# A copy-bound rotation kernel: the first two stores cut into 2 KB pieces

## The chip, the cores and the metric

The kernel runs on one core of a Trainium2 chip. The metric is the time of one execution on the device in microseconds (us), quoted as the median of several runs. The span of a profiled run is the time from its first to its last instruction. Engines named below are VectorE (DVE in the profile), ScalarE's queue (ACTq, which issues the stores here), SyncE's queue (SPq, which issues the loads), and the 16 DMA engines that move the bytes.

All differences here are below 2%, most below 0.5%, so every experiment was timed in five rounds beside runs of the kernel before on the same chip (both_short and loads_short have four timings on record, the others five).

## The reference, cut to what matters

```python
batch, c, h, w = 32, 3, 256, 256
x = np.random.randn(batch, c, h, w).astype(np.float32)

def reference(x):
    return np.rot90(x, k=-1, axes=(-2, -1)).astype(np.float32)
```

Every image of 256 x 256 is rotated by 90 degrees. There is no arithmetic: 25.17 MB are read, rearranged and written.

## The kernel before

The work is cut into 24 slabs of 1 MB. A slab lies on 128 partitions with 2048 floats, 8 KB, in each. A slab is loaded, transposed by two VectorE instructions, and stored. Loads are issued by SyncE and stores by ScalarE, and the trace has them on two DMA queues, of 25.17 MB each: q1 has the loads (first packet at 1.8 us) and q10 the stores (first packet at 13.9 us).

```python
R = 8
n_slabs = B * C * G // P          # 24
PARTS = 2
CP = R // PARTS
...
in_pool = ctx.enter_context(tc.tile_pool(name="in_pool", bufs=12))
out_pool = ctx.enter_context(tc.tile_pool(name="out_pool", bufs=12))

for n in range(n_slabs):
    t_in = in_pool.tile([P, R * W], fp32, tag="t_in")
    nc.sync.dma_start(out=t_in, in_=ld_v[n])

    t_out = out_pool.tile([P, R * W], fp32, tag="t_out")
    src = t_in.rearrange("p (r g c) -> p c r g", r=R, c=R)
    dst = t_out.rearrange("p (c g r) -> p c r g", c=R, r=R)[:, :, ::-1, ::-1]
    for k in range(PARTS):
        cs = slice(k * CP, (k + 1) * CP)
        nc.vector.transpose(out=dst[:, cs], in_=src[:, cs])

    nc.scalar.dma_start(out=st_v[n], in_=t_out)
```

## Time and profile before

| | before |
|---|---|
| time, median (range) | 124.83 us (124.66 to 124.93, 6 runs) |
| span of the profiled run | 122.9 us |
| moved | 50.34 MB, half read from and half written to HBM |
| VectorE busy | 94.6 us (77%) |
| DMA engines | full from the second slice to the last but one, at about 427 GB/s |

The lines below are from the profile's page of the kernel before: the busy digits of VectorE and of the DMA engines in 40 slices of 3.07 us, the traffic in each slice, and the packet count.

```profile
DVE  0199999999897697796977967979769779797500
...
DMA  2999999999999999999999999999999999999994
GB/s 93 427 427 403 339 424 427 427 429 427 427 432 427 427 427 427 432 429 427 427 427 427 429 427 427 427 427 429 427 427 427 427 429 427 427 429 427 427 424 171
DMA packets 6913, 50.34 MB, mean 410 GB/s; under 512 B 768, under 2 KB 768, under 8 KB 768
```

The DMA row is at 9 almost everywhere while VectorE has gaps, so data movement is the bound. And "busy" is not "at full rate": in the slices 4 and 5 the DMA row still shows 9 but only 403 and 339 GB/s move. The same stretch in windows of 1 us (columns: window, its length, busy time of VectorE and of GpSimd with their instruction counts, granted clock, DMA busy share, GB/s; a packet counts whole in the window in which it starts, so a share can exceed 1):

```profile
11.00:12.00 1.00, 1.00 (x2) 0.00 (x0) 1.00 0.94 360
12.00:13.00 1.00, 1.00 (x1) 0.00 (x0) 1.00 1.06 311
13.00:14.00 1.00, 1.00 (x2) 0.00 (x0) 1.00 0.96 287
14.00:15.00 1.00, 1.00 (x1) 0.00 (x0) 1.00 0.94 393
```

This is where the stores join the loads. The first store was issued at 9.67 us and its first packet starts at 13.9 us. Against 427 GB/s, 323 of the 357 GB/s x us that are missing lie before 14 us, so it is the loads that lose, before the first store packet is on record. I call this the dip. Who waited for whom on VectorE (columns: waiter, what it waited for, us in total, times, longest):

```profile
DVE t_out L51 <- DMA t_in<-in_x_dram: 15.4, 12, 5.7
DVE t_out L51 <- DVE t_out L51: 5.4, 6, 0.9
```

### The profile page before, as it was taken

What the parts mean: (1) busy time and instruction counts of PE and PEld (TensorE: products, weight loads), DVE (VectorE), ACT (ScalarE), POOL (GpSimd) and SP (SyncE); (2) the same over time, 40 slices, a digit from 0 to 9 for tenths busy, and PEclk for the clock granted to TensorE, in tenths of its full rate; (3) what the DMA queues carried; (4) which work ended last, traced back from release to release, by engine and by line L of the source; (5) the groups of instructions that cost most, each with busy time, mean ns of one, the idle gap of its engine ahead of it and who ended that gap; (6) DMA issues with size and microseconds to landing.
All of it is one profiled execution on the core that took longest, in us unless ns stands there. A gap on an engine that the chain in (4) does not pass through costs nothing.

```text
span 122.9 us, 186 instructions
## 1 busy us (share of the span) xinstructions
DVE 94.6 (77%) x48; POOL 0.2 (0%) x4
## 2 busy tenths in 40 slices
DVE  0199999999897697796977967979769779797500
POOL 0000000000000000000000000000000000000000
DMA  2999999999999999999999999999999999999994
GB/s 93 427 427 403 339 424 427 427 429 427 427 432 427 427 427 427 432 429 427 427 427 427 429 427 427 427 427 429 427 427 427 427 429 427 427 429 427 427 424 171
DMA packets 6913, 50.34 MB, mean 410 GB/s; under 512 B 768, under 2 KB 768, under 8 KB 768
## 3 DMA queue, kind: packets, MB, share of 16 engines
q1 hardware_dynamic: 3456, 25.17, 49.2%
q10 hardware_dynamic: 3456, 25.17, 48.5%
q14 instruction: 1, 0.01, 0.0%
HBM read 25.17 MB, written 25.17 MB: 410 GB/s over the span
## 4 chain that ended last, share of the span: by engine, by line
DMA 89%; DVE 2%; DVEq 2%; SPq 1%; issue 0%
DMA t_in<-in_x_dram 89%; DVE t_out L51 2%; DVEq L79 2%; SPq L44 1%; DVEq L51 0%
## 5 line engine op out<-in xcount | busy, mean ns | idle before, releaser
L51 DVE STREAM_TRANSPOSE t_out<-t_in 128x1024 f32<-128x1024 f32 x48 | 94.6, 2052 | 20.9 <-DMA t_in<-in_x_dram 15.4
L68 POOL MEMSET const-uint8-127<- 128x1 uint8 x1 | 0.1, 102 | 0.0
L68 POOL MEMSET const-bfloat16-1.0<- 128x1 bf16 x1 | 0.1, 101 | 0.0
L68 POOL MEMSET const-float32-0.0<- 128x1 f32 x1 | 0.1, 98 | 0.2 <-issue 0.2
L68 POOL MEMSET const-float32-1.0<- 128x1 f32 x1 | 0.1, 98 | 0.0
## 6 DMA issues: line engine op xcount, KB each, us to landing
t_in<-in_x_dram SPq DMA_DIRECT2D x24, 1024.0 KB, 19.6
out_dram<-t_out ACTq DMA_DIRECT2D x24, 1024.0 KB, 16.5
```

The source lines that it names most:

```text
L44: nc.sync.dma_start(out=t_in, in_=ld_v[n])
L51: nc.vector.transpose(out=dst[:, cs], in_=src[:, cs])
L68: nc = _bacc.Bacc("TRN2", target_bir_lowering=False, num_devices=1)
L79: with _tile.TileContext(nc) as tc:
```

## The change

The first two stores are to go out as 512 packets of 2 KB each instead of 128 packets of 8 KB; a packet is what the trace records as one transfer of a DMA engine, and `max_dma_last_dim` limits its length in bytes. The likely intent is that the early loads get ahead of the early stores. The limit of 8 KB on the other stores changes nothing, as their rows are 8 KB long.

```diff
     PARTS = 2
+    SHORT = 2
...
-        nc.scalar.dma_start(out=st_v[n], in_=t_out)
+        nc.scalar.dma_start(out=st_v[n], in_=t_out,
+                            max_dma_last_dim=2048 if n < SHORT else 8192)
```

## The prediction

> **What bounds the kernel now.** The data movement. The page gives 50.34 MB in a span of 122.9 us, and in its 40 slices the DMA row is at 9 from the second slice to the last but one, at about 427 GB/s; VectorE is busy 94.6 us (77%). The chain of waits is 89% loads. In the trace nearly every 8 KB packet took 309 ns, 26.5 GB/s on one of 16 engines, 424 GB/s on all. 50.33 MB at 427 GB/s are 117.9 us. The other 5 us are: about 1.8 us before the first load packet, a ramp of the first loads (packets of 350 to 540 ns until about 2.8 us), a dip at the first store, and 1.3 us after the last store packet at 121.6 us.
>
> The dip is the only loss that the change can reach. In windows of 1 us the traffic is 360, 311, 287 and 393 GB/s from 11 to 15 us; load packets take up to 640 ns there. Against 427 this loses 357 GB/s x us, or 0.84 us. The first store was issued at 9.67 us, but its first packet starts only at 13.9 us.
>
> **What the change does.** A row of a store is 8 KB, so the limit of 8 KB on stores 2 to 23 changes nothing. Stores 0 and 1 become 512 packets of 2 KB each instead of 128 of 8 KB: 768 more packets, 48 on each engine. The 4-byte semaphore packets took 9 ns, so I estimate (309-9)/4+9 = 84 ns for 2 KB, and 48 x 9 ns = 0.43 us of additional engine time. Engine time is the bound, so this lies wholly on the critical path.
>
> **What it moves.** [...] loads get about 4/5 of the bytes while the short stores run: the mixed traffic of one load and one store packet is 309 + 84 ns. Stores 0 and 1 would then land much later (the first lands at 19.3 us now; I expect 25 to 30, the second 35 to 40), loads 4 to 10 sooner (near 3.2 to 3.5 us apart instead of 4.9), and VectorE would run without waits in that stretch. Stores pile up and drain at the end: the last loads land some 8 to 12 us before the 111.3 us of now, VectorE ends by about 105 us. That buys no time, because already now the engines stay full to the end (stores alone move 427 GB/s from 111 to 121 us).
>
> **Sum.** +0.4 us for packets, and between 0 and -0.84 us for the dip; I guess that short pieces, whose first packets finish sooner, take away most of it. Net about -0.2 us: 124.6 us. Range 123.7 to 125.4. Chances: faster by over 2% 0.02, within 2% 0.95, slower by over 2% 0.03.
>
> **What would show it.** Packets rise from 6913 to about 7681. 2 KB packets of 80 to 100 ns confirm the packet cost. The windows from 11 to 15 us: above 400 GB/s if the dip goes, near 340 if it stays. VectorE's wait for loads (15.4 us in total now) falls and the last load lands earlier if the sharing is by packet; unchanged if not.
>
> **What would make it wrong.** 2 KB packets that take much longer than 84 ns (each 10 ns more costs 0.64 us); short pieces that keep loads from starting, so that VectorE starves; stores so late that their buffers hold up VectorE; or a dip that grows.

Read the 4/5 as the assumption that the two queues take turns packet by packet. Whether they do is read from the trace of the changed kernel (607 load packets of 8 KB beside 672 store packets of 2 KB from 18 to 33 us, so 0.78 of the bytes were the loads'). The sum is +0.4 us for packets and about -0.6 us, most of the 0.84 us, for the dip, which gives the net of -0.2 us.

## The result, and the profile after

| | before | after |
|---|---|---|
| time, median of 6 runs | 124.83 us | 124.52 us (124.31 to 124.80) |
| ratio of the fast runs | | 0.9978, 95% interval 0.9964 to 0.9993 |
| span of the profiled run | 122.9 us | 122.8 us |
| VectorE's wait for loads | 15.4 us | 7.9 us |
| last load landed | 111.3 us | 98.2 us |
| last store packet ended | 121.6 us | 121.6 us |

A ratio is the mean time of one kernel's fast runs over that of the other's fast runs of the same rounds, so it is not quite the ratio of the medians. The changed kernel is faster by about 0.2%, which is within 2%.

The same lines of the page, after the change:

```profile
DVE  0199999999999999999999999897796693000000
...
DMA  3999999999999999999999999999999999999993
GB/s 93 422 427 427 393 427 422 415 420 432 426 408 411 427 427 427 427 427 427 427 427 430 427 427 427 427 427 430 427 430 427 427 427 430 424 427 427 427 430 163
DMA packets 7681, 50.34 MB, mean 410 GB/s; under 512 B 768, under 2 KB 768, under 8 KB 1792
```

VectorE now runs without a gap until the 25th slice and is done 13 us sooner, and the execution ends at the same place all the same: the DMA engines are full to the end, now with stores alone. The slice at the dip rises from 339 to 393 GB/s. But slices 12 and 13 fall to 408 and 411. The dip in windows of 1 us, after the change:

```profile
11.00:12.00 1.00, 1.00 (x2) 0.00 (x0) 1.00 0.95 401
12.00:13.00 1.00, 1.00 (x1) 0.00 (x0) 1.00 1.01 385
13.00:14.00 1.00, 1.00 (x2) 0.00 (x0) 1.00 1.04 401
14.00:15.00 1.00, 1.00 (x1) 0.00 (x0) 1.00 0.96 389
```

And a second, smaller dip, which the prediction did not have. It is where the last 2 KB packet (36.5 us) gives way to the first 8 KB store packet (36.4 us):

```profile
35.00:36.00 1.00, 1.00 (x1) 0.00 (x0) 1.00 0.95 397
36.00:37.00 1.00, 1.00 (x2) 0.00 (x0) 1.00 1.16 399
37.00:38.00 1.00, 1.00 (x1) 0.00 (x0) 1.00 0.95 393
38.00:39.00 1.00, 1.00 (x2) 0.00 (x0) 1.00 1.01 426
```

The page counts packets by size, and the difference, 7681 - 6913 = 768, is the 768 more that four pieces for one make of 256 rows. VectorE's waits after the change:

```profile
DVE t_out L54 <- DMA t_in<-in_x_dram: 7.9, 4, 5.6
DVE t_out L54 <- DVE t_out L54: 1.8, 2, 0.9
```

**How losses are measured below.** What one packet costs an engine follows from calm stretches of the traces, as 16 x the stretch over the packets that started in it. An 8 KB packet costs 306.4 ns (60 to 95 us, before). With that subtracted for the loads' 8 KB packets, a 4 KB packet of a store costs 155.9 ns, a 2 KB packet 80.5 ns and a 1 KB packet 42.3 ns. The "loss" in a window is its length less the cost of the packets moved in it, per engine; a packet on an edge counts by the part of its recorded duration that lies inside. So short packets are paid in their cost, and the loss shows the dip alone. (The expectations below count 0.24 us, or about 4 ns for each of 64 packets on an engine, for two stores in 2 KB pieces; that agrees with 64 x 80.5 - 16 x 306.4 ns = 0.25 us.) The "join" is the time when the stores begin beside the loads, the "step" the time when the short store packets give way to 8 KB. In windows of 9 us around the join the loss before is 0.82 us; after it is 0.21 us, and 0.22 us more in the 6 us around the step from 2 KB to 8 KB.

### The profile page after: what moved, and what is told of

It is laid out like the page before. It is cut to its first block, busy times and chain, and to the rows that moved or that the text cites. A ratio compares the mean times of both kernels' runs of the same rounds, so it can differ in the third digit from the quotient of the medians.

```text
span 122.8 us, 186 instructions
## 1 busy us (share of the span) xinstructions
DVE 92.5 (75%) x48; POOL 0.2 (0%) x4
## 2 busy tenths in 40 slices
DMA packets 7681, 50.34 MB, mean 410 GB/s; under 512 B 768, under 2 KB 768, under 8 KB 1792
## 4 chain that ended last, share of the span: by engine, by line
DMA 72%; DVE 8%; DVEq 2%; SPq 1%; issue 0%
DMA t_in<-in_x_dram 72%; DVE t_out L54 8%; DVEq L83 2%; SPq L47 1%; DVEq L54 0%
## 5 line engine op out<-in xcount | busy, mean ns | idle before, releaser
L54 DVE STREAM_TRANSPOSE t_out<-t_in 128x1024 f32<-128x1024 f32 x48 | 92.5, 2047 | 9.7 <-DMA t_in<-in_x_dram 7.9
```

## The experiments

The theories were these:

- **D**: the gain comes from the smaller dip at the join of stores and loads; the packets are a cost.
- **P**: the gain comes from the preference for loads (0.78 of the bytes after the join in the changed kernel), which keeps VectorE fed, wherever it is given.
- **C**: the dip is a cold start of the first writes of a program.
- **Z**, a narrow form of D: only the size of the store's packets sets the dip.
- **S**: the dip is larger the larger the share of the bytes that the stores take when they join, whatever packet sizes give that share.

All twelve runs gave correct results. Every edit is shown against the changed kernel, that of hold_real against hold_stores. "Before" stands for the runs of the kernel before on the same chip: 124.71 us for the first four kernels, 124.82 us for the second four, 124.69 us for the last four.

### The changed kernel again (after_again)

No edit.

> The changed kernel once more, on the chip of the three runs below. Both theories: 0.3 us under before, about 124.5 us; loss against 427 GB/s about 0.2 us from 11 to 15 us and about 0.2 us from 35.5 to 39 us.

Measured: 124.44 us, ratio 0.9976 (0.9964 to 0.9989). The loss at the join was 0.23 us and at the step 0.36 us. The gain is real and repeats; the loss at the step varies from run to run (0.22 and 0.36 us).

### Short stores in the middle (mid_short)

```diff
-                            max_dma_last_dim=2048 if n < SHORT else 8192)
+                            max_dma_last_dim=2048 if n in (10, 11) else 8192)
```

> 2 KB pieces in stores 10 and 11 instead of 0 and 1. Theory D (the gain is the smaller dip when stores join loads, and 2 KB packets cost about 4 ns each, 0.24 us for two stores): the dip of 0.8 us from 11 to 15 us is back in full, the packets are paid, and there may be a dip of 0.2 us at the step from 2 KB to 8 KB; about +0.3 to +0.5 us on before, 125.2 us. Theory P (the gain is that loads get 4/5 of the engines for a while and VectorE waits less, wherever that is): VectorE's wait falls by some 5 us and the time falls to about 124.5 us.

Measured: 124.82 us, ratio 1.0008 (0.9995 to 1.0020). Below are VectorE's waits in this kernel, and after them two windows of its join:

```profile
DVE t_out L54 <- DMA t_in<-in_x_dram: 10.7, 7, 5.7
DVE t_out L54 <- DVE t_out L54: 0.9, 1, 0.9
```

```profile
9.00:12.00 3.00, 3.00 (x3) 0.00 (x0) 1.00 1.00 399
12.00:15.00 3.00, 3.00 (x2) 0.00 (x0) 1.00 1.00 336
```

This decides against P. VectorE waited 4.7 us less for loads than before (15.4 us), and the kernel gained nothing. The join lost 0.82 us, exactly as before. The expectation of theory D was 0.3 to 0.5 us over before; the median is 0.11 us over, and the interval of the ratio has 1 in it, so the size didn't hold and the direction isn't shown. The steps to 2 KB and back to 8 KB in the middle (at 62.8 and 86 us) lost 0.01 and 0.00 us. The packet cost of 0.25 us (worked out below) is at the upper edge of the interval.

### Held stores, which did not hold (hold_stores)

```diff
+        outs.append(t_out)
+        if n == 2:
+            nc.vector.tensor_copy(out=outs[0][:, 0:1], in_=outs[0][:, 0:1])
+        if n >= 2:
+            for m in ((0, 1, 2) if n == 2 else (n,)):
+                nc.scalar.dma_start(out=st_v[m], in_=outs[m])
-        nc.scalar.dma_start(out=st_v[n], in_=t_out, ...)
```

> All stores in 8 KB pieces, but store 0 is held back until the third slab is transposed (a copy of one column on VectorE makes it wait), then stores 0, 1 and 2 go out together. Loads have the engines to themselves for 8 us longer. Theory D: the dip moves to about 19 to 23 us and keeps its 0.8 us, so the time is that of before, 124.8 us. Theory P: VectorE waits less, as with the change, so about 124.5 us. Theory C (the dip is a cold start of some kind, of the first write of a program): same as D here.

Measured: 124.66 us, ratio 0.9994 (0.9981 to 1.0006), and the first store was issued at 9.6 us, as before. The experiment failed: the copy depends only on slab 0, so it was scheduled right after slab 0. It serves only as another run of the kernel before: the loss at the join was 0.80 us.

### Held stores, second try (hold_real)

The copy is replaced by one that needs the third slab (its value is unchanged, as zero is added):

```diff
-            nc.vector.tensor_copy(out=outs[0][:, 0:1], in_=outs[0][:, 0:1])
+            nc.vector.scalar_tensor_tensor(out=outs[0][:, 0:1], in0=outs[2][:, 0:1], scalar=0.0,
+                                           in1=outs[0][:, 0:1], op0=mybir.AluOpType.mult,
+                                           op1=mybir.AluOpType.add)
```

> The held stores again; the first try did not hold them (its copy was put right after the first slab). Now one column of store 0 is rewritten from the third slab, times zero, so the first store cannot go out before about 17.3 us; all stores in 8 KB pieces. Theory S (the dip is what the join of stores to running loads costs, larger the larger the stores' share of the bytes): the dip moves to about 19 to 23 us at 0.8 us, the time is that of before, 124.8 us. Theory P (the gain is loads ahead and VectorE waiting less): VectorE waits less and the time is about 124.5 us. If the dip belongs to a fixed time of the program, it stays at 11 to 15 us.

Measured: 124.74 us, ratio 1.0005 (0.9991 to 1.0019). The first store was issued at 13.3 us (presumably store 1, which went first of the three), so the hold was 3.6 us instead of 7.6 us. The first store packet started at 17.5 us instead of 13.9, and the dip moved with it. First come the windows of before, three of 3 us each:

```profile
9.00:12.00 3.00, 3.00 (x3) 0.00 (x0) 1.00 1.00 410
12.00:15.00 3.00, 3.00 (x2) 0.00 (x0) 1.00 0.99 330
15.00:18.00 3.00, 3.00 (x3) 0.00 (x0) 1.00 1.00 423
```

Then those of the kernel with held stores:

```profile
12.00:15.00 3.00, 3.00 (x2) 0.00 (x0) 1.00 1.02 426
15.00:18.00 3.00, 3.00 (x4) 0.00 (x0) 1.00 0.98 300
18.00:21.00 3.00, 3.00 (x3) 0.00 (x0) 1.00 1.00 421
```

The dip belongs to the join and not to a time of the program; the loss in 9 us around it was 0.90 us. VectorE's wait for loads did not fall (17.5 us), so this run says nothing on P; mid_short does that. It does not separate C from S either, since the held store was still the program's first.

### Short loads beside the short stores (both_short)

```diff
-        nc.sync.dma_start(out=t_in, in_=ld_v[n])
+        nc.sync.dma_start(out=t_in, in_=ld_v[n],
+                          max_dma_last_dim=2048 if 3 <= n <= 7 else 8192)
```

> As the change, and loads 3 to 7 are in 2 KB pieces as well, so that load and store packets are equal while the short stores start and the loads have no preference. Seven short transfers cost 7 x 0.12 = 0.84 us of packets instead of 0.24. Theory D: the dip at 11 to 15 us stays small (0.2 us), time about 125.1 us. If the dip shrank only because loads had the preference: it is back at 0.6 to 0.8 us, time about 125.7 us.

Measured: 126.24 us, ratio 1.0118 (1.0103 to 1.0134). The first two stores are in 2 KB pieces as in the changed kernel, but the windows of this kernel show the dip again:

```profile
9.00:12.00 3.00, 3.00 (x3) 0.00 (x0) 1.00 0.99 377
12.00:15.00 3.00, 3.00 (x2) 0.00 (x0) 1.00 1.01 330
```

The loss at the join was 0.65 us (the packets are paid in their cost). The loads' own change to 2 KB, at 9.9 us, is not the reason: from 9 to 11 us the loss was 0.00 us. So the size of the store's packets does not set the dip, and theory Z falls, together with my first reading of D. What differs is how the two queues share the bytes: the stores have 0.50 of them here and 0.22 in the changed kernel. The time is worse than either expectation because the late loads starved the end: 360 GB/s from 117 to 120 us, a loss of 0.38 us, and after 120 us another 0.52 us more than before.

### Other sizes (one_short, four_kb, one_kb)

```diff
-    SHORT = 2                                                    # one_short
+    SHORT = 1
-                            max_dma_last_dim=2048 if n < SHORT else 8192)
+                            max_dma_last_dim=4096 if n < SHORT else 8192)   # four_kb
+                            max_dma_last_dim=1024 if n < SHORT else 8192)   # one_kb
```

> Only store 0 in 2 KB pieces. Theory D: the dip at 11 to 15 us is as small as with two (0.2 us), the packet cost halves to 0.12 us, and the dip at the step to 8 KB comes at about 25 us instead of 36: about 0.1 us under the changed kernel, 124.4 us. Theory P: half of the preference, so half of the gain, 124.65 us.

Measured: 124.66 us, ratio 0.9988 (0.9975 to 1.0000). Join 0.32 us, step 0.31 us (at 25 us). D expected a larger gain than with two short stores, and none shows (the intervals overlap): join, step and packets (0.12 us) sum to 0.75 us in this profile and to 0.21 + 0.22 + 0.25 = 0.68 us in that of the change. The 124.65 us of P were met; it is mid_short that decides against P.

> Stores 0 and 1 in 4 KB pieces. If the dip is in proportion to the piece [...]: 0.4 us at 11 to 15 us, packets 0.08 us, and a dip of 0.1 to 0.4 us at the step to 8 KB; 124.5 to 124.8 us.

Measured: 124.56 us, ratio 0.9979 (0.9966 to 0.9993). Join 0.56 us, step 0.05 us. The time is as expected, but the loss at the join is more than the 0.4 us of a dip in proportion to the piece.

> Stores 0 and 1 in 1 KB pieces. If the dip is in proportion to the piece: 0.1 us at 11 to 15 us; packets 128 per engine more than with 2 KB at 4 ns, so 0.24 + 0.5 us; the step to 8 KB comes later (loads get 8/9) and costs 0.2 to 0.7 us; about 125.0 us.

Measured: 124.51 us, ratio 0.9974 (0.9962 to 0.9987). Join 0.07 us, step 0.01 us. The expected time of 125.0 us was missed by 0.5 us, as the packets cost less than the 0.74 us allowed and the step, for which 0.2 to 0.7 us were allowed, cost nothing. With 1 KB pieces the dip is gone from the windows:

```profile
9.00:12.00 3.00, 3.00 (x3) 0.00 (x0) 1.00 1.03 434
12.00:15.00 3.00, 3.00 (x2) 0.00 (x0) 1.00 1.02 420
15.00:18.00 3.00, 3.00 (x3) 0.00 (x0) 1.00 1.01 413
```

It is no faster than the change because it pays more for packets. Its two short stores are 128 packets on each engine, 128 x 42.3 ns, where 16 packets of 8 KB would do, 16 x 306.4 ns: 0.51 us more. For the changed kernel the same sum is 64 x 80.5 - 16 x 306.4 ns = 0.25 us.

### A short first load (load0_short)

```diff
-        nc.sync.dma_start(out=t_in, in_=ld_v[n])
+        nc.sync.dma_start(out=t_in, in_=ld_v[n],
+                          max_dma_last_dim=2048 if n < 1 else 8192)
```

> As the change, and load 0 in 2 KB pieces. The loads lose 0.87 us in their own start (1.7 to 4 us). If starting a stream costs in proportion to the packet, that falls to 0.2 to 0.4 us and the time to about 124.2 us; if it is the latency of the first bytes, it stays and the time is 124.6 us (packets 0.12 us).

Measured: 124.50 us, ratio 0.9977 (0.9965 to 0.9990), the same as the change. The first 9 us lose 2.69 us, against 2.62 us with the change alone (some 1.8 us of both pass before the first packet): the start of the loads is not shortened by shorter packets. Join 0.24 us; the step at 37 us lost 0.03 us here, against 0.22 and 0.36 us in the changed kernel.

### Short loads, full stores (loads_short)

Loads 3 to 7 as in both_short, and `max_dma_last_dim=8192` on all stores.

> Loads 3 to 7 in 2 KB pieces, all stores in 8 KB pieces: the stores get 4/5 when they join. Theory S, from the losses by share so far (1/9: 0.04, 1/5: 0.20, 1/3: 0.49, 1/2: 0.81 us): over 1 us at 11 to 16 us. Theory Z (only the size of the store's packets counts): 0.8 us. Packets cost 0.6 us besides. Loads fall behind and may starve VectorE and the end: 126 us or more, so read the windows, not the time.

Measured: 127.00 us, ratio 1.0189 (1.0175 to 1.0203), which is "unclear" at the limit of 2%. The windows of the join in this kernel:

```profile
9.00:12.00 3.00, 3.00 (x3) 0.00 (x0) 1.00 1.02 385
12.00:15.00 3.00, 3.00 (x2) 0.00 (x0) 1.00 1.03 277
15.00:18.00 3.00, 3.00 (x3) 0.00 (x0) 1.00 0.99 412
```

The loss at the join was 1.24 us, the largest of all, as S expected and Z did not. From 9 to 11 us, after the loads' change to 2 KB at 9.6 us, it was 0.00 us. (The losses that the expectation quotes lie a little under those of the table below, in the same order.)

### One store in 1 KB pieces, and a graded start (one_kb_once, graded)

```diff
-                            max_dma_last_dim=2048 if n < SHORT else 8192)
+                            max_dma_last_dim=1024 if n == 0 else 8192)      # one_kb_once
```

> Store 0 alone in 1 KB pieces. Theory S: dip at the join 0.04 us, packets 0.26 us (half of the 0.52 us of two such stores); the step to 8 KB at about 33 us costs from 0 (as after two 1 KB stores) to 0.3 us (as after one 2 KB store). 124.3 to 124.6 us; loss at the step decides.

Measured: 124.53 us, ratio 0.9987 (0.9975 to 1.0000). Join 0.10 us, but the step from 1 KB to 8 KB at 34 us lost 0.58 us, twice what I allowed for.

```diff
+        pieces = {0: ((0, 512, 1024), (512, 2048, 2048)), 1: ((0, 2048, 4096),)}
+        for lo, hi, piece in pieces.get(n, ((0, 2048, 8192),)):
+            nc.scalar.dma_start(out=st_v[n][:, lo:hi], in_=t_out[:, lo:hi],
+                                max_dma_last_dim=piece)
-        nc.scalar.dma_start(out=st_v[n], in_=t_out, ...)
```

> A try at the best of it: the first quarter of store 0's rows in 1 KB pieces, its rest in 2 KB, store 1 in 4 KB, the others in 8 KB. Theory S with small steps: join 0.04 us, packets 0.06 + 0.09 + 0.05 us, each step under 0.1 us: 124.2 us, 0.5 to 0.6 us under before. If steps cost what shares say in sum (0.8 us less what one step saves), 124.7 us.

Measured: 124.44 us, ratio 0.9982 (0.9970 to 0.9995). Join 0.14 us; the three steps lost 0.02, 0.06 and 0.29 us. The edit also moves the join: a quarter of store 0 needs only the first transpose, so it was issued at 7.7 us instead of 9.6 us. The hoped 124.2 us were not reached. No version here beats the change clearly: the intervals of four_kb, one_kb, load0_short and graded all overlap with its own.

### The losses together

The share is that of the stores in the bytes moved after the join, counted from the trace; where it was not counted separately it is that of the kernel with the same packet sizes.

| load / store packet at the join | share of the stores | kernels | loss at the join, us |
|---|---|---|---|
| 8 KB / 1 KB | 0.12 | one_kb, one_kb_once, graded | 0.07, 0.10, 0.14 |
| 8 KB / 2 KB | 0.22 | after, after_again, load0_short, one_short | 0.21, 0.23, 0.24, 0.32 |
| 8 KB / 4 KB | 0.35 | four_kb | 0.56 |
| 2 KB / 2 KB | 0.50 | both_short | 0.65 |
| 8 KB / 8 KB | 0.50 | before, mid_short, hold_stores, hold_real | 0.82, 0.82, 0.80, 0.90 |
| 2 KB / 8 KB | 0.72 | loads_short | 1.24 |

The loss at the join rises with the share of the stores, over the whole range, whichever side's packets are changed. That much is shown. At the same share of 0.50 it is a little smaller with 2 KB packets on both sides, so the share is not all of it. Theory C in its plain form falls, as an edit of loads alone moved the loss from 0.82 to 1.24 us; but every join tried was the first of its program, and the later rises of the share in mid_short (at 86 us) and in both_short (at 24 us, from about 0.5 to 0.8) lost nothing. So what is shown of the share holds for the first join only, and that it must be the first join may still be a part of the cause. What an engine does in those 3 us is not: the traces show only that load packets stretch from 309 to as much as 834 ns, and that the first store packet starts 3.5 to 4.3 us after its store was issued.

The loss at a later step up to 8 KB is not settled. With loads in 8 KB pieces it was 0.58, 0.36, 0.31, 0.29 and 0.22 us in five cases (between 25 and 37 us), and 0.05 us or less in four others (at 28, 37, 54 and 86 us). Neither the height of the step nor its time sorts them: 1 KB to 8 KB lost 0.58 us in one_kb_once and 0.01 us in one_kb.

## Why the prediction was right or wrong

The time was predicted as 124.6 us within 123.7 to 125.4, and was 124.52 us; "within 2%" was given 0.95 and came. Point by point:

- **The bound.** Right. VectorE's waits fell by half, the last load landed 13 us sooner, and the last store packet ended at 121.6 us in both kernels. mid_short shows the same separately.
- **The packet records.** Right as a reading: 2 KB packets took 84 ns in the records, as estimated. **But the cost was mis-sized**: "48 x 9 ns = 0.43 us of additional engine time" took the recorded durations for engine time. Records of neighbouring packets overlap a little: 8 KB packets recorded at 309 ns follow each other every 306.4 ns, and 2 KB packets recorded at 84 ns cost 80.5 ns. The two stores cost 0.25 us more, not 0.43 us. For each packet that is added the runs show (4 x 80.5 - 306.4)/3 = 5.2 ns with 2 KB, (8 x 42.3 - 306.4)/7 = 4.6 ns with 1 KB. (They rest on small differences: in other calm stretches a 2 KB packet cost 78.9 to 81.7 ns, which makes 3 to 7 ns.)
- **The sharing by packet.** Right. After the join the stores have 0.22 of the bytes, near the 1/5 predicted. Turns of one packet, which the prediction assumed, are what the traces show: from 18 to 33 us of the changed kernel 607 load packets of 8 KB ran beside 672 store packets of 2 KB, and in one_kb (18 to 48 us) 1356 beside 1513 of 1 KB. Counts alone would also fit longer turns, but a store packet started 3 or 4 ns before the end of 594 of the 607 load packets, and of 1340 of the 1356. The first store landed at 25.6 us (25 to 30 predicted) and the second at 37.2 us (35 to 40). Loads landed about 3.2 us apart (3.2 to 3.5). The last load was 13.2 us sooner (8 to 12 predicted, so a little more), and VectorE's last transpose ended at 102.3 us ("by about 105").
- **The dip.** The size of the gain was right, the reason was half right. "I guess that short pieces, whose first packets finish sooner, take away most of it": the loss at the join fell from 0.82 to 0.21 us. But both_short has the same short store packets and lost 0.65 us. What the runs show is the share of the stores, not their packets' size as such.
- **What was missing.** A second dip of 0.22 to 0.36 us at the return to 8 KB. It was not in the sum, and hid the packet cost that was overestimated: two errors of about 0.2 us with opposite signs, so that the sum came out near is in part luck.

The sum by the traces is therefore -0.61 us at the join, +0.25 us for packets and +0.22 to +0.36 us at the step: between -0.14 us and zero. That fits the executions that were profiled: they took 124.67 us before and 124.59 us after, and their spans differ by 0.07 us. The medians differ by more, 0.31 and 0.27 us in 6 and 5 runs, and what they gain beyond the sum, 0.15 to 0.3 us, lies in executions of which no trace was kept, so I could not place it. One source of scatter is seen: after 120 us the profiles of before and of the changed kernel lose 1.71, 1.76 and 1.55 us. mid_short lost 1.52 us there, and so was 0.10 us over before in span, although its packets cost 0.25 us. The parts are shown one by one; the size of the gain in the medians is not accounted for in full.

## What to carry to other kernels

Where the DMA engines are full from end to end, feeding a compute engine sooner bought nothing here (VectorE was done 13 us sooner, and the last store packet ended at 121.6 us all the same); look in the windows for stretches that are busy but move fewer bytes. Here such a stretch came where a second queue joined a running one, and smaller packets on the joining side made it smaller (0.82 to 0.21 us), as the two queues took turns packet by packet and the joining one got fewer bytes (0.22 of them instead of 0.50); but each packet costs (0.25 us here for two stores in 2 KB pieces), and a part of what is saved may come back at the step to large packets (0.22 and 0.36 us in two runs of the changed kernel). Cost packets by how many fit in a calm stretch (306.4 ns for 8 KB here), not by their recorded durations (309 ns).
